# A decoder step on one core: the compressed-key branch, two sequences per weight block

## The chip, the cores and the metric

The kernel runs on one core of a Trainium2 chip. The metric is the device time of one execution in microseconds. The engines named below are PE (matrix products), PEld (its weight loads), DVE (vector), ACT (activations and copies), POOL (general purpose, here also the issuer of gathers and of some transfers) and SP (issuer of most transfers). Each engine executes its own instructions in program order and waits in place for whatever an instruction needs.

## The reference, cut to what matters

One inference step of a small trunk: a 512-token prompt and 8 decode sequences of 4 tokens go through a convolution module and a SwiGLU feed-forward layer (FFN), then through sparse attention and a second FFN. The part that the change rewrites is `compress` for the decode sequences. Each of the 8 sequences has 1024 cached rows in pages; every 32 rows are flattened with their 64 values (a vector of 2048), for keys (e=0) and values (e=1) and 4 heads, and pass a two-layer perceptron:

```python
def compress(kv_full, w_phi1, b_phi1, w_phi2, b_phi2, pe_cmp):
    blk = kv_full[:, :n * CMP_BLOCK].reshape(B, n, CMP_BLOCK, 2, KV_HEADS, HEAD_DIM)
    blk = blk + pe_cmp.transpose(1, 0, 2)[:, :, None, :]
    blk = blk.transpose(0, 1, 3, 4, 2, 5).reshape(B, n, 2, KV_HEADS, CMP_BLOCK * HEAD_DIM)
    hid = jax.nn.silu(jnp.einsum('bnegf,efh->bnegh', blk, w_phi1) + b_phi1[:, None, :])
    out = jnp.einsum('bnegh,ehd->bnegd', hid, w_phi2) + b_phi2[:, None, :]
```

Per sequence and e that is 32 blocks x 4 heads = 128 columns against a 2048 x 128 weight, so 16 weight blocks of 128 x 128, in fp32. The position term `pe_cmp` is the same for all columns; it is multiplied with the weights once and becomes part of the bias `bh`.

## The kernel before, in words

The program is written as one stream of calls per stage; a scheduler that ships with the language orders each engine's instructions by priority and by its own estimate of when inputs are ready. The stages that matter here, in order: the convolution (DVE chains of 31 taps, some channels on PE); its layer norm (`layer_norm_out`: the sum of the channels at L814 on PE, the centred rows `y` at L820 on DVE, their squares on ACT and the sums of these at L814 on PE, root, reciprocal, then `h_hi`/`h_lo` at L831/L832); the product with `w_pw2` (8 blocks of L183/L185 at 256 and 288 columns, called pw2 below); the norm before the FFN; and the first FFN with units j=0 to 7 (a gate and an up product, L183/L185 at 272 columns; the pair is joined at L915 on DVE, rounded at L921 on ACT, and the rest `a_lo` is made at L922 on POOL), then the product with the first part of `w_down` (called down below), which reads `a_hi` and `a_lo` of units 0 to 7 in turn, and so on. Slabs of `w_ada` (L451 load, L453 product) are strewn in between.

The compressed branch is a generator, `compress_steps`. All its steps are drawn in one go under a very low priority (`high_priority(-LATER)`) and behind the last tap of the convolution's DVE chains (`issue_after(self.last_step)`); MID is 24, the number of its steps, so all of it is drawn. By this the scheduler fills it into gaps of the stages above. Per sequence b and half hp: a gather on POOL (L1032, 1 MB into one of two `nat` tiles), two DVE transposes (L1045) into the `xt` tiles of keys and values; then per e a chain of 16 products (L1051: stationary weight block, 128 moving columns), for b=0 another 16 with one column for the bias (L1055), Silu on ACT (L1059), and a small second product (L1062 for keys, L1068 for values) with its bias on DVE (L1066, L1071); the values' rows go to DRAM from POOL (L1072). A PE call in fp32 shows as two instructions in the trace, so a chain is 32. The accumulators come from the two banks `t`.

Behind the branch, in the pool of SBUF that it gives back, the bias tables are made (`bias_tables`: L1092 and L1117 on PE, the transfers line_r, line_f and bs_d at L1099, L1096, L1121 on POOL), and then the selected and window keys are moved (`key_steps`: gather kr at L1032 on POOL into one of two tiles, v_d at L1301 on SP, transposes ktr at L1306 on DVE, kt_d at L1309 on SP; 24 steps of about 1 to 2 MB of traffic).

Of the kernel before, what the change touches and what calls it, by code (L numbers as in the profile page):

```python
# [7 lines left out]
F32 = mybir.dt.float32  # L8
F32R = mybir.dt.float32r
I32 = mybir.dt.int32  # L10
AF = mybir.ActivationFunctionType
# [14 lines left out]
G = 4  # L26
# [27 lines left out]
MID = 24  # L54
# [59 lines left out]
class Kernel:  # L114
# [883 lines left out]
    def compress_loads(self, pool):  # L998
# [21 lines left out]
        pe = pool.tile([P, P], F32, name="hk", bufs=2)[:, :HD]  # L1020
# [13 lines left out]
    def compress_steps(self, pool):  # L1034


        v, s, g, te = self.v, self.s, self.g, self.te
        self.compress_loads(pool)
        for b in range(NB):
            xts = [self.shift_pool.tile([P, 8, 8, 32], F32, name="xt", bufs=3) for _ in range(2)]  # L1040
            for hp in range(2):
                nat = pool.tile([P, 4, 512], F32, name="nat", bufs=2)
                self.load_rows(nat.rearrange("p t e -> p (t e)"), self.A["cache_kv_cmp"], hp, b)
                for e in range(2):
                    v.transpose(xts[e][:, hp * 4:hp * 4 + 4].rearrange("p s q n -> p s (q n)"), nat[:, :, e * 256:(e + 1) * 256])  # L1045
                yield
            for e in range(2):
                xv = xts[e].rearrange("p s (g h) n -> p h s g n", h=2)
                ph = self.bank()
                for c in range(16):  # L1050
                    te.matmul(ph[:, :P], self.w1[:, e, c // 2, c % 2], xv[:, c % 2, c // 2], start=c == 0, stop=c == 15)  # L1051
                if b == 0:
                    pb = self.bank()
                    for c in range(16):
                        te.matmul(pb[:, :1], self.w1[:, e, c // 2, c % 2], self.peT[:, c % 2, e * 8 + c // 2:e * 8 + c // 2 + 1],  # L1055
                                  start=c == 0, stop=c == 15)
                    v.tensor_scalar(self.bh[:, e:e + 1], pb[:, :1], self.b_phi1[:, e:e + 1], None, op0=ALU.add)
                hk = pool.tile([P, P], F32, name="hk", bufs=2)
                s.activation(hk, ph[:, :P], AF.Silu, bias=self.bh[:, e:e + 1])  # L1059
                po = self.bank()  # L1060
                if e == 0:
                    te.matmul(po[:, :P], self.w2k, hk, start=True, stop=True)  # L1062
                    pv = po[:, :P].rearrange("p (q g n) -> p q g n", q=2, g=2)
                    for g2 in range(2):
                        sl = slice(g2 * HD, (g2 + 1) * HD)
                        v.tensor_scalar(self.cks[sl, b], pv[sl, :, g2], self.b2k[sl], None, op0=ALU.add)  # L1066
                else:
                    te.matmul(po[:, :HD], hk, self.w2v, start=True, stop=True)  # L1068
                    cv = pool.tile([32, 256], F32, name="cv", bufs=1)
                    for gg in range(G):  # L1070
                        v.tensor_tensor(out=cv[:, gg * HD:(gg + 1) * HD], in0=po[gg * 32:(gg + 1) * 32, :HD], in1=self.b2v[:32], op=ALU.add)  # L1071
                    g.dma_start(self.vtail[b, 0:32], cv)  # L1072
            yield
        self.dump("cks", self.cks)
# [573 lines left out]
    def run(self):  # L1648
# [5 lines left out]
        with sbuf("const") as self.cp, sbuf("norm") as self.np, \  # L1654
# [17 lines left out]
            with sbuf("conv") as pool:  # L1672
# [18 lines left out]
                with tc.high_priority(-LATER):  # L1691
                    for _ in between:
                        pass
                    with tc.issue_after(self.last_step):
                        for _ in range(MID):
                            next(compress)
                    self.conv_states(pool)
# [120 lines left out]
```

## Time and profile before

| | us |
|---|---|
| median of 3 runs | 1673.56 (1667.45 to 1677.68) |
| the profiled execution's own time | 1666.48 |
| its span in the profile | 1664.7 |
| PE busy in that span | 1562.4 |
| DVE / ACT / POOL busy | 1109.1 / 696.1 / 230.5 |

Times inside the execution count from the start of the span. PE is busy for 94% of it, but the share differs by stage, and a busy PE may run at half its clock: the column PEclk is the granted clock as a share of 2.4 GHz, so a mean of 0.8 means that a part of the stretch ran at the lower level of 1.2 GHz. The chain of waits lists what ended last, step by step, with start and duration; "x32" there counts instructions, and the duration of a merged row over its count is the pace.

### The profile page before, as it was taken

To read this page: it belongs to the slowest core of one execution; us is meant where nothing else is said; L and a number is where in the kernel's file an instruction comes from. 1 tells how busy PE (TensorE), PEld (TensorE's weight loads), DVE (VectorE), ACT (ScalarE), POOL (GpSimd) and SP (SyncE) were. 2 spreads that over 40 slices of the span, in tenths; PEclk is the share of its full clock that TensorE was granted. 3 is DMA by queue.
4 is the path that set the end of the run, shared out by engine and by line. 5 is a ranking of instruction groups with operands and counts; after the bars stand their busy time and mean duration, and the time that the engine had idled before them with its cause. 6 is when DMAs were issued, how large, how long until landed. Compare 5 with 4: busy or idle time off the path is not lost.

```text
span 1664.7 us, 31621 instructions
## 1 busy us (share of the span) xinstructions
PE 1562.4 (94%) x12423; PEld 1372.3 (82%) x12423; DVE 1109.1 (67%) x2369; ACT 696.1 (42%) x1443; POOL 230.5 (14%) x270
## 2 busy tenths in 40 slices
PE   6989889999989978999999899999999999999997
PEld 3976468899979868999878677655699999999997
DVE  2899855464457877687656634867856864884865
ACT  5411145322132433155445322756746542652554
POOL 3254310111121112001120000000011110110010
PEclk8989888999999999999999999999999999999998
DMA  9729662653389999835689885847222472333231
GB/s 309 213 66 249 184 198 88 216 166 128 118 215 329 317 290 314 277 107 113 180 259 275 257 246 180 228 149 231 56 65 76 152 228 86 91 114 90 79 91 64
DMA packets 315568, 295.26 MB, mean 177 GB/s; under 512 B 16019, under 2 KB 275485, under 8 KB 311179
## 3 DMA queue, kind: packets, MB, share of 16 engines
q1 hardware_dynamic: 304507, 237.24, 48.3%
q0 software_dynamic: 10224, 55.47, 10.4%
q8 instruction: 98, 1.61, 0.4%
q10 hardware_dynamic: 688, 0.53, 0.1%
q14 instruction: 51, 0.42, 0.1%
HBM read 256.28 MB, written 45.48 MB: 181 GB/s over the span
## 4 chain that ended last, share of the span: by engine, by line
PE 65%; DMA 15%; DVE 12%; issue 4%; ACT 2%; SPq 1%; POOL 0%; ACTq 0%; DVEq 0%; POOLq 0%
PE g L185 16%; PE g L183 15%; PE g L247 10%; PE t L247 3%; DMA raw<-in_w_ada_dram 3%; PE t L155 3%; PE t L1051 3%; DMA raw<-in_w_gate_dram 2%; PE o L1532 2%; DVE wlo L196 2%; DVE y L770 2%; DMA raw<-in_w_down_dram 1%; PE a L453 1%; PE t L1381 1%; DVE wlo L170 1%
## 5 line engine op out<-in xcount | busy, mean ns | idle before, releaser
L169 ACT CAST whi<-raw 128x512 fp32r<-128x512 f32 x250 | 149.4, 605 | 394.1 <-PE g L185 287.1
L170 DVE TENSOR_TENSOR wlo<-raw,whi 128x512 fp32r<-128x512 f32 x250 | 174.9, 705 | 142.2 <-ACT whi L169 132.7
L183 PE MATMUL g<-h_hi,whi 128*128 128x256 f32 (+1 forms) x584 | 172.7, 297 | 12.8 <-DVE un L682 7.9
L185 PE MATMUL g<-h_lo,whi 128*128 128x288 f32 (+4 forms) x584 | 175.3, 300 | 0.6 <-DVE h_lo L577 0.6
L185 PE MATMUL g<-h_hi,whi 128*128 128x288 f32 (+4 forms) x584 | 174.9, 300 | 0.9 <-ACT h_hi L576 0.9
L185 PE MATMUL g<-h_hi,wlo 128*128 128x288 f32 (+4 forms) x584 | 174.5, 299 | 0.0
L183 PE MATMUL g<-h_lo,whi 128*128 128x256 f32 (+1 forms) x584 | 168.8, 289 | 0.4 <-DVE h_lo L562 0.4
L183 PE MATMUL g<-h_hi,wlo 128*128 128x256 f32 (+1 forms) x584 | 168.9, 289 | 0.0
L183 PEld LDWEIGHTS g<-h_hi,whi 128*128 128x128 f32 x584 | 113.1, 194 | 28.9 <-issue 17.0
L247 PE MATMUL g<-T,whi 128*128 128x272 f32 x656 | 126.9, 289 | 2.7 <-DVE ht L261 1.2
L195 ACT CAST whi<-s 128x512 fp32r<-128x512 f32 x128 | 79.4, 621 | 111.0 <-PE g L247 61.0
L183 PEld LDWEIGHTS g<-h_hi,wlo 128*128 128x128 f32 x584 | 113.0, 193 | 4.3 <-issue 4.2
L185 PEld LDWEIGHTS g<-h_hi,whi 128*128 128x128 f32 x584 | 113.1, 194 | 3.3 <-issue 2.1
L183 PEld LDWEIGHTS g<-h_lo,whi 128*128 128x128 f32 x584 | 113.1, 194 | 3.1 <-issue 2.4
L185 PEld LDWEIGHTS g<-h_lo,whi 128*128 128x128 f32 x584 | 112.4, 192 | 3.3 <-issue 2.3
L183 PE MATMUL g<-a_hi,whi 128*128 128x256 f32 (+1 forms) x372 | 107.1, 288 | 7.7 <-DVE x L641 3.1
L185 PEld LDWEIGHTS g<-h_hi,wlo 128*128 128x128 f32 x584 | 112.6, 193 | 1.2 <-issue 1.2
L185 PE MATMUL g<-a_hi,wlo 128*128 128x288 f32 (+1 forms) x372 | 110.5, 297 | 0.0
L185 PE MATMUL g<-a_hi,whi 128*128 128x288 f32 (+1 forms) x372 | 110.2, 297 | 0.0
L183 PE MATMUL g<-a_lo,whi 128*128 128x256 f32 (+1 forms) x372 | 105.2, 283 | 5.0 <-POOL a_lo L922 5.0
L185 PE MATMUL g<-a_lo,whi 128*128 128x288 f32 (+1 forms) x372 | 109.8, 296 | 0.0
L196 DVE TENSOR_TENSOR wlo<-s,whi 128x512 fp32r<-128x512 f32 x128 | 88.7, 697 | 26.4 <-ACT whi L195 22.3
(512 smaller groups left out, 4154.3 us busy)
## 6 DMA issues: line engine op xcount, KB each, us to landing
raw<-in_w_ada_dram SPq DMA_DIRECT2D x76, 512.0 KB
raw<-in_w_gate_dram SPq DMA_DIRECT2D x44, 512.0 KB
raw<-in_w_up_dram SPq DMA_DIRECT2D x44, 512.0 KB
raw<-in_w_down_dram SPq DMA_DIRECT2D x32, 512.0 KB
raw<-in_w_pw_dram SPq DMA_DIRECT2D x24, 512.0 KB
kt_d<-ktr SPq DMA_DIRECT2D x96, 128.0 KB
kt<-kt_d SPq DMA_DIRECT2D x24, 512.0 KB
xt<-in_w_ada_dram SPq DMA_DIRECT2D x20, 512.0 KB
```

Source lines behind the costliest of these rows:

```text
L155: self.te.transpose(out, in_, self.ident[:n, :n])
L169: self.s.copy(hi[:, :b - a], raw[:, a:b])
L170: self.v.tensor_tensor(out=lo[:, :b - a], in0=raw[:, a:b], in1=hi[:, :b - a].bitcast(F32), op=ALU.subtract)
L183: self.last_product = self.te.matmul(pg[:, 0, :split], a, b[:, i, :split], start=st, stop=sp).ins
L185: self.te.matmul(pg[:, 1, :tokens - split], a, b[:, i, split:tokens], start=st, stop=sp)
L195: self.s.copy(hi, src)
L196: self.v.tensor_tensor(out=lo, in0=src, in1=hi.bitcast(F32), op=ALU.subtract)
L247: self.te.matmul(out, a[:, i], b(i), start=first and i == 0 and j == 0, stop=i == 3 and j == 2, skip_group_check=not first)
L453: self.te.matmul(pa[32 * j:32 * j + 32, :256], self.cT[:, k, :], w[:, j * 256:(j + 1) * 256], start=k == 0, stop=k == KT - 1)
L770: self.last_step = v.scalar_tensor_tensor(out=ps, in0=x, scalar=w, in1=ps, op0=ALU.mult, op1=ALU.add).ins
L1051: te.matmul(ph[:, :P], self.w1[:, e, c // 2, c % 2], xv[:, c % 2, c // 2], start=c == 0, stop=c == 15)
L1532: te.matmul(po[rp * HD:(rp + 1) * HD, :256], self.vn[:, br, t, gg * HD:(gg + 1) * HD], pT[:, rp * 256:(rp + 1) * 256], start=br == 0 and t ...
```

## The change

Two sequences go through the branch together. Both gathers of a half are issued, the two sequences' transposes write one `xt` tile per half and e, and each weight block meets 256 columns in one call: 128 calls of 256 columns (L1065) take the place of 256 calls of 128. Two accumulators are held through both halves. Silu and the keys' second product take 256 columns at a time; the values' second product stays at 64 columns, twice. The bias is made first, by 32 calls with `peT` as the stationary side (one column) and the weights as 128 moving columns (L1042), a copy of the row on ACT and two transposes on PE. The tile `hk` has one buffer of twice the size in the place of two. MID goes away: the generator is still drawn whole at the same place, under the same priority. Line numbers behind the constants fall by one, those behind the branch rise by 12.

The diff:

```diff
--- before.py
+++ after.py
@@ -51,7 +51,6 @@
 STATE = 2
 LAST = KT - 1
 ORDER = (0, 1, 2, 3, 4, 5, 6, 7)
-MID = 24
 PE_CONV = (3, 4, 5, 6, 7)
 
 BUCKET_START = [16, 21, 27, 35, 46, 59, 77, 99, 128, 166, 216, 280, 363, 470, 609, 790]
@@ -1017,7 +1016,7 @@
         self.b2v = cp.tile([P, HD], F32, name="b2v")
         self.sy.dma_start(self.b2v, A["b_phi2"][1].rearrange("(o d) -> o d", o=1).broadcast_to([P, HD]))
         self.bh = cp.tile([P, 2], F32, name="bh")
-        pe = pool.tile([P, P], F32, name="hk", bufs=2)[:, :HD]
+        pe = pool.tile([P, 2, P], F32, name="hk", bufs=1)[:, 0, :HD]
         self.v.memset(pe, 0.0)
         src = A["pe_cmp"].rearrange("e (a s) d -> a e s d", a=4)
         for a in range(4):
@@ -1036,40 +1035,53 @@
 
         v, s, g, te = self.v, self.s, self.g, self.te
         self.compress_loads(pool)
-        for b in range(NB):
-            xts = [self.shift_pool.tile([P, 8, 8, 32], F32, name="xt", bufs=3) for _ in range(2)]
+
+        pb = self.bank()
+        for e in range(2):
+            for c in range(16):
+                te.matmul(pb[:1, e * P:(e + 1) * P], self.peT[:, c % 2, e * 8 + c // 2:e * 8 + c // 2 + 1], self.w1[:, e, c // 2, c % 2],
+                          start=c == 0, stop=c == 15)
+        row = pool.tile([P, 2, P], F32, name="hk", bufs=1)[:1]
+        s.copy(row, pb[:1, :2 * P].rearrange("p (e n) -> p e n", e=2))
+        pb = self.bank()
+        for e in range(2):
+            self.transpose(pb[:, e:e + 1], row[:, e])
+        v.tensor_tensor(out=self.bh, in0=pb[:, :2], in1=self.b_phi1, op=ALU.add)
+        yield
+
+        for b in range(0, NB, 2):
+            phs = [self.bank() for _ in range(2)]
             for hp in range(2):
-                nat = pool.tile([P, 4, 512], F32, name="nat", bufs=2)
-                self.load_rows(nat.rearrange("p t e -> p (t e)"), self.A["cache_kv_cmp"], hp, b)
+                nats = [pool.tile([P, 4, 512], F32, name="nat", bufs=2) for _ in range(2)]
+                for i in range(2):
+                    self.load_rows(nats[i].rearrange("p t e -> p (t e)"), self.A["cache_kv_cmp"], hp, b + i)
                 for e in range(2):
-                    v.transpose(xts[e][:, hp * 4:hp * 4 + 4].rearrange("p s q n -> p s (q n)"), nat[:, :, e * 256:(e + 1) * 256])
+                    xt = self.shift_pool.tile([P, 2, 4, 8, 32], F32, name="xt", bufs=3)
+                    for i in range(2):
+                        v.transpose(xt[:, i].rearrange("p s q n -> p s (q n)"), nats[i][:, :, e * 256:(e + 1) * 256])
+                    xv = xt.rearrange("p i s (g h) n -> p s h i g n", h=2)
+                    for c in range(8):
+                        k = 4 * hp + c // 2
+                        te.matmul(phs[e][:, :2 * P], self.w1[:, e, k, c % 2], xv[:, c // 2, c % 2], start=hp == 0 and c == 0, stop=hp == 1 and c == 7)
                 yield
             for e in range(2):
-                xv = xts[e].rearrange("p s (g h) n -> p h s g n", h=2)
-                ph = self.bank()
-                for c in range(16):
-                    te.matmul(ph[:, :P], self.w1[:, e, c // 2, c % 2], xv[:, c % 2, c // 2], start=c == 0, stop=c == 15)
-                if b == 0:
-                    pb = self.bank()
-                    for c in range(16):
-                        te.matmul(pb[:, :1], self.w1[:, e, c // 2, c % 2], self.peT[:, c % 2, e * 8 + c // 2:e * 8 + c // 2 + 1],
-                                  start=c == 0, stop=c == 15)
-                    v.tensor_scalar(self.bh[:, e:e + 1], pb[:, :1], self.b_phi1[:, e:e + 1], None, op0=ALU.add)
-                hk = pool.tile([P, P], F32, name="hk", bufs=2)
-                s.activation(hk, ph[:, :P], AF.Silu, bias=self.bh[:, e:e + 1])
+                hk = pool.tile([P, 2, P], F32, name="hk", bufs=1)
+                s.activation(hk.rearrange("p i n -> p (i n)"), phs[e][:, :2 * P], AF.Silu, bias=self.bh[:, e:e + 1])
                 po = self.bank()
                 if e == 0:
-                    te.matmul(po[:, :P], self.w2k, hk, start=True, stop=True)
-                    pv = po[:, :P].rearrange("p (q g n) -> p q g n", q=2, g=2)
+                    te.matmul(po[:, :2 * P], self.w2k, hk.rearrange("p i n -> p (i n)"), start=True, stop=True)
+                    pv = po[:, :2 * P].rearrange("p (i q g n) -> p i q g n", i=2, q=2, g=2)
                     for g2 in range(2):
                         sl = slice(g2 * HD, (g2 + 1) * HD)
-                        v.tensor_scalar(self.cks[sl, b], pv[sl, :, g2], self.b2k[sl], None, op0=ALU.add)
+                        v.tensor_scalar(self.cks[sl, b:b + 2], pv[sl, :, :, g2], self.b2k[sl], None, op0=ALU.add)
                 else:
-                    te.matmul(po[:, :HD], hk, self.w2v, start=True, stop=True)
-                    cv = pool.tile([32, 256], F32, name="cv", bufs=1)
-                    for gg in range(G):
-                        v.tensor_tensor(out=cv[:, gg * HD:(gg + 1) * HD], in0=po[gg * 32:(gg + 1) * 32, :HD], in1=self.b2v[:32], op=ALU.add)
-                    g.dma_start(self.vtail[b, 0:32], cv)
+                    for i in range(2):
+                        te.matmul(po[:, i * HD:(i + 1) * HD], hk[:, i], self.w2v, start=True, stop=True)
+                    for i in range(2):
+                        cv = pool.tile([32, 256], F32, name="cv", bufs=1)
+                        for gg in range(G):
+                            v.tensor_tensor(out=cv[:, gg * HD:(gg + 1) * HD], in0=po[gg * 32:(gg + 1) * 32, i * HD:(i + 1) * HD], in1=self.b2v[:32], op=ALU.add)
+                        g.dma_start(self.vtail[b + i, 0:32], cv)
             yield
         self.dump("cks", self.cks)
 
@@ -1692,8 +1704,8 @@
                     for _ in between:
                         pass
                     with tc.issue_after(self.last_step):
-                        for _ in range(MID):
-                            next(compress)
+                        for _ in compress:
+                            pass
                     self.conv_states(pool)
                 self.layer_norm_out(pool, acc, ada1)
             self.dump("x1", self.x)
```

The scheduler sets all engines' order anew. Three places:

PE, from the end of the convolution to the first product of pw2 (`ada_sb`, `raw,cT`: slabs of w_ada; `acc`, `sq`: the layer norm's sums; `g<-h_hi`: pw2). Before:

```order
L814 MATMUL g<-sq,ones 128x272 x14
L453 MATMUL a<-raw,cT 32x256 x4
L1062 MATMUL t<-hk,w2k 128x128
L1051 MATMUL t<-xt,w_1958 128x128 x6
L814 MATMUL g<-sq,ones 128x272 x2
L1051 MATMUL t<-xt,w_1958 128x128 x10
L1055 MATMUL t<-peT,w_1958 128x1 x6
L453 MATMUL a<-raw,cT 32x256 x4
L1055 MATMUL t<-peT,w_1958 128x1 x10
L453 MATMUL a<-raw,cT 32x256 x4
L183 MATMUL g<-h_hi,whi 128x256
```

and now:

```order
L1042 MATMUL t<-w_1958,peT 1x128 x8
L813 MATMUL g<-sq,ones 128x272 x2
L452 MATMUL a<-raw,cT 32x256 x4
L1042 MATMUL t<-w_1958,peT 1x128
L813 MATMUL g<-sq,ones 128x272 x2
L1042 MATMUL t<-w_1958,peT 1x128 x4
L154 MATMUL t<-c_small,hk 128x1 x2
L1065 MATMUL t<-xt,w_1958 128x256 x9
L452 MATMUL a<-raw,cT 32x256 x4
L1065 MATMUL t<-xt,w_1958 128x256 x13
L182 MATMUL g<-h_hi,whi 128x256
L184 MATMUL g<-h_hi,whi 128x288
```

Behind the norm's last sum there now stand 22 calls of 256 columns ahead of pw2, where 10 of 128 and 16 bias calls stood; the bias calls stand between the sums of squares, and nothing of the branch stands ahead of the first sum. Over the whole program the 256-column calls stand 22 ahead of pw2, 18 within it, 24 between it and the FFN, and 64 in the FFN ahead of down; the 128-column calls stood 32, 11, 37 and 176.

POOL, around the hand-over from the branch to the keys in the first FFN (`a_lo` rows are units 6 and 7 before, and units 5, 6 and 7 now). Before:

```order
L922 TENSOR_TENSOR a_lo<-ht,a_hi 128x544
L1099 DMA line_r<-lsb 512x1x320 x2
L1096 DMA line_f<-lsb 16x512 x2
L1121 DMA bs_d<-bs 4x32x394 x2
L1032 DMA kr<-in_cache_kv_sel_dram,rows_78 128x2048 x2
L922 TENSOR_TENSOR a_lo<-ht,a_hi 128x544
L1032 DMA kr<-in_cache_kv_sel_dram,rows_78 128x2048 x6
```

and now:

```order
L1111 DMA line_r<-lsb 512x1x320 x2
L1108 DMA line_f<-lsb 16x512 x2
L921 TENSOR_TENSOR a_lo<-ht,a_hi 128x544
L1133 DMA bs_d<-bs 4x32x394 x2
L1031 DMA kr<-in_cache_kv_sel_dram,rows_78 128x2048 x2
L921 TENSOR_TENSOR a_lo<-ht,a_hi 128x544
L1031 DMA kr<-in_cache_kv_sel_dram,rows_78 128x2048
L921 TENSOR_TENSOR a_lo<-ht,a_hi 128x544
L1031 DMA kr<-in_cache_kv_sel_dram,rows_78 128x2048 x7
```

Two gathers stood ahead of the last `a_lo` (unit 7); now three stand ahead of it, and two ahead of that of unit 6. On PE the first product of the bias tables stands 195 products of L183/L185 ahead of down now, and 78 before.

DVE, at the same place (`ht<-ht,g` joins a unit: unit 7 before, units 6 and 7 now). Before:

```order
L915 TENSOR_TENSOR ht<-ht,g 128x544
L949 TENSOR_TENSOR sg<-h_hi,h_lo 128x544
L170 TENSOR_TENSOR wlo<-raw,whi 128x512
L272 TENSOR_TENSOR sg<-sg 128x272
L273 SCALAR_TENSOR_TENSOR sg<-sg 128x272
L278 TENSOR_TENSOR h_lo<-sg,h_hi 128x272
L274 SCALAR_TENSOR_TENSOR sg<-sg 128x272
L949 TENSOR_TENSOR sg<-h_hi,h_lo 128x544
L170 TENSOR_TENSOR wlo<-raw,whi 128x512
L1306 STREAM_TRANSPOSE ktr<-kr 128x4x4x32 x2
```

and now:

```order
L914 TENSOR_TENSOR ht<-ht,g 128x544
L169 TENSOR_TENSOR wlo<-raw,whi 128x512
L1318 STREAM_TRANSPOSE ktr<-kr 128x4x4x32 x2
L169 TENSOR_TENSOR wlo<-raw,whi 128x512
L1318 STREAM_TRANSPOSE ktr<-kr 128x4x4x32 x2
L169 TENSOR_TENSOR wlo<-raw,whi 128x512
L277 TENSOR_TENSOR h_lo<-sg,h_hi 128x272
L948 TENSOR_TENSOR sg<-h_hi,h_lo 128x544
L271 TENSOR_TENSOR sg<-sg 128x272
L272 SCALAR_TENSOR_TENSOR sg<-sg 128x272
L169 TENSOR_TENSOR wlo<-raw,whi 128x512
L277 TENSOR_TENSOR h_lo<-sg,h_hi 128x272
```

The first transposes of the keys stood behind the join of unit 7; now two pairs stand between those of units 6 and 7.

## Rows read from the trace of the kernel before

**Rows 1.** The page, part 1: busy time and share of the span by engine.

```profile
PE 1562.4 (94%) x12423; PEld 1372.3 (82%) x12423; DVE 1109.1 (67%) x2369; ACT 696.1 (42%) x1443; POOL 230.5 (14%) x270
```

**Rows 2.** Windows by stage: length, busy (instructions) by engine, PEclk, DMA share, GB/s.

```profile
215.50:254.70 39.20, 33.52 (x216) 26.97 (x216) 19.43 (x27) 17.14 (x25) 2.56 (x3) 0.81 0.60 199
254.70:312.40 57.70, 57.66 (x462) 55.31 (x463) 28.00 (x57) 21.02 (x34) 0.57 (x1) 0.95 0.37 116
312.40:330.90 18.50, 16.48 (x128) 14.74 (x128) 10.65 (x21) 9.35 (x16) 4.91 (x5) 0.82 0.92 285
330.90:480.50 149.60, 148.47 (x1219) 141.64 (x1217) 79.06 (x138) 40.23 (x74) 29.43 (x36) 1.00 0.49 141
480.50:491.30 10.80, 5.78 (x48) 5.54 (x44) 4.50 (x9) 2.23 (x4) 3.38 (x3) 0.88 0.99 238
491.30:695.00 203.70, 185.00 (x1427) 172.51 (x1428) 150.76 (x253) 69.01 (x133) 26.37 (x22) 0.96 0.99 316
```

**Rows 3.** The same windows for the chains alone (L1051): PE, PEld, PEclk, DMA.

```profile
215.50:254.70 39.20, 10.98 (x64) 10.44 (x64) 0.81 0.60 199
...
312.40:330.90 18.50, 11.00 (x74) 10.88 (x74) 0.82 0.92 285
330.90:480.50 149.60, 43.70 (x355) 41.41 (x353) 1.00 0.49 141
```

**Rows 4.** The chain of waits, paces: start, duration, engine, tile, line, instructions.

```profile
228.16 2.57 PE t L1055 x24
243.12 0.93 PE g L814 x4
...
405.63 3.57 PE t L1051 x32
...
426.36 3.63 PE t L1051 x32
```

**Rows 5.** The chain of waits from the first slab to pw2.

```profile
222.26 0.94 PE a L453 x8
...
226.03 0.57 PE a L453 x8
...
227.24 0.92 PE g L814 x4
...
244.07 0.72 ACT rstd L825
...
248.29 2.31 DVE xt L1045 x2
...
254.74 0.58 PE g L183
```

**Rows 6.** The chain of waits, norm before the FFN and bias tables.

```profile
320.17 5.87 PE t L1051 x32
...
467.29 1.02 PE t L1092 x8
```

**Rows 7.** Timeline of POOL at the keys: start, us, instruction, idle before.

```profile
470.31 1.04 POOL L1096 DMA_DIRECT2D line_f<-lsb  x2
...
487.57 1.05 POOL L1032 DMA_INDIRECT kr<-in_cache_kv_sel_dram,rows  x1 [10.32 <-DMA line_f<-lsb]
488.93 0.98 POOL L1032 DMA_INDIRECT kr<-in_cache_kv_sel_dram,rows  x1 [0.30 <-issue]
489.93 1.35 POOL L922 TENSOR_TENSOR a_lo<-ht,a_hi 128x544 fp32r<-128x544 f32 x1
509.10 1.33 POOL L1032 DMA_INDIRECT kr<-in_cache_kv_sel_dram,rows  x1 [17.82 <-DVE x L643]
```

**Rows 8.** Timeline of PE, the resumed product of down.

```profile
491.33 0.58 PE L183 MATMUL g<-a_lo,whi 128*128 128x256 f32 x1 [5.05 <-POOL a_lo L922]
```

**Rows 9.** Timeline of DVE, the first transposes of the keys.

```profile
495.79 2.02 DVE L1306 STREAM_TRANSPOSE ktr<-kr 128x512 f32<-128x512 f32 x2 [6.03 <-DMA kr<-in_cache_kv_sel_dram,rows]
```

## The prediction

> **What bounds the kernel now.** I read the page's first part, then windows by stage, then the chain of waits inside two of the stages, and last the timelines of POOL, PE and DVE where the keys begin. The first part says PE: 94% busy [rows 1]. So time falls only where PE works less, idles less, or runs longer at the upper of its two levels (1.2 and 2.4 GHz). The windows [rows 2] say where that is possible. In the FFN (330.9 to 480.5) nothing is lost: 148.5 of 149.6 us busy at clock 1.00. Before pw2 (215.5 to 254.7) PE idles 5.7 us and its clock is 0.81; pw2's stage runs at 0.95; the norm's gap (312.4 to 330.9) has 2.0 us idle at 0.82. From 491.3 to 695, DMA is 0.99 busy and PE loses 18.7 us idle and 4% of its clock, 8.1 us more: 26.8 us. The branch's chains lie in all stages up to 480.5: in instructions 64, 74 and 355 of those windows [rows 3], the rest in pw2's stage. Wherever PE is full, what the branch costs it is paid one for one.
>
> **The chains.** 32 instructions take 3.57 to 3.63 us at full clock, 0.1125 each [rows 4]; 256 calls are 512 instructions, 57.6 us. No row shows an fp32 call with 256 columns and a full weight block. Bounds: the one-column bias calls move nothing yet take 2.57/24 = 0.107 per instruction; the norm's sums move 272 fp32 columns at 0.93/4 = 0.2325 [rows 4]. If only the weight load counted, 128 calls would take 256 x 0.1125 = 28.8 us (a saving of 28.8; the FFN's products, rounded to fp32r and one instruction each, do come at 0.127 with 272 columns, worked out below); at the price of 272 columns 59.5 us (a loss of 1.9). I take 0.2325 x 256/272 = 0.219, nearest in columns and type: 0.436 us per call, 55.8 us, a saving of 1.8. Half the calls, nearly the same time.
>
> The Trainium skill speaks for the low bound: "TensorE: Matmul & The Clock Gate", section "Back-to-back issue gap", gives a warm matmul N/2.4 + 2.5 ns, an estimate of 109 ns for 256 columns, and its section "LDWEIGHTS (loading the stationary operand)" P/1.2, 107 ns for 128. By both, the chains would cost about 28 us. The trace does not agree for this type: 0.2325 us at 272 columns is twice that formula.
>
> **The bias.** Still 32 calls, 64 instructions, 0.107 each by the weight load: 7 us before and after. A sum of 128 columns would be at most 0.1125, 0.4 us more. The row's copy on ACT and two transposes of one column lie beside the sums; the single `hk` orders ACT behind PE's second layer, which other products cover. The second layer moves the same columns: zero. `cv` still has one buffer, so the second sequence's adds on DVE wait for the first's transfer, in the FFN, where PE is not waiting for DVE; without that cover some 2 us, four times.
>
> **Up to pw2.** The order puts 56 bias instructions among the norm's sums where 32 stood, and takes 14 of the branch's other products away: 24 x 0.107 - 14 x 0.1125 = +1.0 us. DVE also makes `peT` behind the centred rows; between nothing and 2.3 us by the transposes of [rows 5]. I take the last sum 2.7 us later, near the top, since DVE is in use there: 245.8 for 243.12 [rows 4]. Against this, the transposes that stood between the reciprocal and `ht` (2.31 us, [rows 5]) leave that path, so `h_hi` is ready 0.4 later, at about 255.1. PE is later than that: behind the sum it has 4 bias calls (0.9), the row's detour (0.7), 22 calls (9.6) and a slab (0.57 [rows 5]): 245.8 + 0.9 + 11.8 = 258.5. pw2 thus begins 3.8 us later than at 254.74 [rows 5], with the idle time ahead of it filled: 22 new calls equal 44 old, where 32 were done.
>
> **pw2 and the norm's gap.** In pw2 18 new calls replace 11: 7.9 - 2.5 = +5.4. Without idle time ahead, the clock should stay up: 57.7 us at 0.95 hold 2.9 us to win [rows 2]; I count all, nothing is the other end. Then 24 calls for 37: 10.5 - 8.3 = +2.1; the second layer +0.4. In the gap the chain shows 32 instructions at 5.87 us instead of 3.6 [rows 6], 2.3 lost, and 2.0 idle [rows 2]; with more of the branch's work at hand both go: -4.3, nothing the other end. FFN at 330.9 + 3.8 + 5.4 - 2.9 + 2.1 + 0.4 - 4.3 = 335.4.
>
> **FFN to down.** 149.6 - 176 x 0.225 + 64 x 0.436 = 137.9: down begins at about 473.3 for 480.5, 7.2 us earlier.
>
> **The keys.** This is the step that decides what remains. Down's products read `a_lo` of unit 7, and PE resumes with it at 491.33 after waiting 5.05 us for POOL [rows 8], about 5.4 us of work into down. POOL was late because its gather waited 10.3 us for line_f, and a second gather and the `a_lo` followed [rows 7]. On PE the bias tables began at 467.29, 13.2 us and 78 products of the FFN ahead of down [rows 2, 6]; by the order 195 products stand there now. Outside the chains the FFN's instructions take (149.6 - 355 x 0.1125)/(1219 - 355) = 0.127 us [rows 2, 3], so the tables begin 13.2 + 117 x 0.127 = 28.1 us before 473.3, at about 445. Their path to the first gather was 487.57 - 467.29 = 20.3 us [rows 6, 7]: first gather at 465.3, 22 us earlier. But now the third gather too stands ahead of unit 7's `a_lo`, and it needs a `kr` tile back: it came 509.10 - 487.57 = 21.5 us after the first [rows 7]. With its own 1.33 and the `a_lo`'s 1.35, PE resumes at 465.3 + 24.2 = 489.5, 1.8 us earlier than before; of the 7.2 us won, 5.4 become a longer wait, 11 us for 5. Bounds: landing (495.79 - 487.57 = 8.2) and transposes (2.0 [rows 9]) alone would free a tile after 10.2 us, and then PE would not wait at all (-12); two turns, 43 us, would make it resume at 511 (+20). DVE's key transposes between the joins wait for that landing too, some 3 us that lie inside the same stall. I take the measured 21.5.
>
> **The DMA-bound stage.** Before, the first gather led the resumption by 3.8 us, now by 24.2: 20.4 of 203.7 us of traffic moves under FFN and stall, 10% of the 26.8 us lost: -2.7. Nothing, and nearly all 26.8, are the ends.
>
> **Sum.** -1.8 - 2.7 = -4.5 against the profiled execution's 1666.48: 1662.0. That execution stands 7.1 us under the median of the runs; against the median the forecast is **1669 us**.
>
> **Rivals.**
> A, nothing is won: the stage after 491 takes the earlier start back because weights and keys share a full DMA. For it: 0.99 [rows 2]. Against: traffic that moved earlier is gone from the stage. About 1674. Chance 0.18.
> B, the saturated stage is relieved: if weights are late only for want of bandwidth, 20 us of traffic done before frees up to 20 us. For it: the idle 18.7 us all lie where DMA is at 0.99 [rows 2]. Against: the keys' pace is set by two `kr` tiles, so they will stretch beside the weights as before. -17 to -26: 1648 to 1657. Chance 0.17.
> C, the change does for PE what the halved calls suggest, weight loads being the cost: -28.8 and part of B, about 1640. The 272-column row speaks against it. Chance 0.05. It is the time that the formulas of the Trainium skill would give.
> D, slower: POOL's third gather stands ahead of the last `a_lo`. It needs `kr` back, whose transfer to DRAM stands on SP behind weights, whose buffers come free only as PE moves on; and PE waits for that `a_lo`. Break-even is a third gather some 26.7 us after the first (4.5 us lost at 0.87); at two turns (43 us) +21.5, less 13% of it given back by the stage: +14 in all, 1688; it passes 1% from about 46 us. For it: 17.8 us of POOL's wait before that gather already [rows 7]. Against: the FFN's DMA is at 0.49 [rows 2], so this turn should be no slower than the measured one. 1678 to 1695. Chance 0.10.
> The forecast has 0.50, within 1661 to 1677.
>
> **How the numbers follow.** A measurement of this kernel tells 1% (16.7 us) from no change, no less. Faster by that, below 1656.8: most of B and all of C, 0.20. Slower, above 1690.3: half of D and a tail, 0.07. The rest, 0.73, is no change. The range leaves out C, the edge of B, and the worse half of D: 1650 to 1682. All term bounds but the chain's low one (C) and the keys' high one (D) lie within it.
>
> **What would show it.** Right: 256-column calls at about 0.436 us; pw2's first product near 258.5, the FFN's near 335, down's near 473; the first gather near 465 and PE then waiting some 11 us for unit 7's `a_lo`, with the third gather just ahead of it; idle time of the next 200 us a little below 18.7. Wrong: calls near 0.22 (C); a stage behind the resumption with less than 8 us idle (B); a third gather more than 27 us behind the first (D); the FFN's start not much later, or down's not earlier, which would break the account of the terms ahead of the keys.

## The result, and the profile after

The changed kernel takes 1654.16 us (median of 9 runs) where the kernel before takes 1670.92 in the same comparison: ratio 0.9907, 95% interval 0.9878 to 0.9936. One of the 9 runs of the kernel before took 5624.93 us and is left out of the ratio. Two further series gave 0.9893 (0.9866 to 0.9920) and 0.9899 (0.9870 to 0.9929). The forecast was 1669 with a range of 1650 to 1682. The time is inside the range, but outside 1661 to 1677, which had half of the chance: the gain of about 16 us, or 1%, is more than three times the 4.5 us that the sum gave.

The page's first part, after, beside [rows 1]:

```profile
PE 1555.1 (94%) x12161; PEld 1354.2 (82%) x12161; DVE 1109.4 (67%) x2360; ACT 693.8 (42%) x1435; POOL 233.6 (14%) x270
```

PE is busy for 7.3 us less, and for the same share of the span. Stages of the profiled execution, as in [rows 2] (length, then busy time and instructions by engine, granted clock, DMA share, GB/s); the stretches are the norm's sums up to pw2, pw2 with the norm's gap, the FFN, the hand-over and the DMA-bound stage:

```profile
230.58:264.26 33.68, 30.57 (x183) 20.73 (x179) 17.99 (x22) 12.83 (x18) 2.05 (x2) 0.97 0.35 100
264.26:340.81 76.55, 76.39 (x578) 69.80 (x576) 46.49 (x85) 27.50 (x45) 9.19 (x11) 1.00 0.64 199
340.81:478.30 137.49, 136.41 (x985) 125.70 (x985) 62.88 (x110) 37.20 (x64) 27.68 (x34) 1.00 0.52 152
478.30:492.57 14.27, 7.73 (x49) 7.08 (x45) 12.51 (x19) 3.12 (x6) 2.62 (x2) 0.87 0.87 261
492.57:690.00 197.43, 182.49 (x1384) 170.50 (x1385) 149.90 (x255) 70.15 (x135) 25.56 (x21) 0.95 0.99 308
```

pw2, its gap and the FFN now run with little idle time (0.2 and 1.1 us) and at a granted clock of 1.00. The pace of the chains, from the chain of waits (the row that answers to [rows 4]):

```profile
413.85 12.09 PE t L1065 x56
```

12.09/56 = 0.216 us per instruction, 0.432 per call: 55.3 us for all 128, where 57.6 stood. Calls near 0.22 us, the sign of rival C, are not there, so C is out. The formula of the Trainium skill ("TensorE: Matmul & The Clock Gate", "Back-to-back issue gap") gives an estimate of 0.109 us for 256 columns, half of the 0.216 us per instruction; the row does not agree.

PE up to pw2, from its timeline (start, us, instruction, idle before and what ended it; the rows answer to [rows 5]):

```profile
229.57 1.08 PE L452 MATMUL a<-raw,cT 128*32 128x256 f32 x8 [6.36 <-DMA raw<-in_w_ada_dram]
230.58 2.18 PE L813 MATMUL g<-acc,ones 128*128 128x272 f32 x4
234.27 2.10 PE L813 MATMUL g<-sq,ones 128*128 128x272 f32 x8 [0.88 <-ACT sq L821]
238.15 1.91 PE L1042 MATMUL t<-w,peT 128*1 128x128 f32 x16 [1.78 <-DVE peT L1026]
251.27 1.19 PE L813 MATMUL g<-sq,ones 128*128 128x272 f32 x4
264.26 0.47 PE L182 MATMUL g<-h_hi,whi 128*128 128x256 f32 x1
```

From the first sum (230.58) to the last (251.27) it takes 20.7 us where it took 15.9: 56 bias instructions now stand between them, at 0.115 us each (the 16 from 238.15 on take 1.84 us), and PE waits 1.78 us for `peT`.

The hand-over, on POOL, DVE and PE (the rows that answer to [rows 7, 8, 9]):

```profile
470.28 1.06 POOL L1031 DMA_INDIRECT kr<-in_cache_kv_sel_dram,rows  x1 [12.49 <-DMA line_f<-lsb]
...
472.64 1.40 POOL L921 TENSOR_TENSOR a_lo<-ht,a_hi 128x544 fp32r<-128x544 f32 x1
489.86 0.96 POOL L1031 DMA_INDIRECT kr<-in_cache_kv_sel_dram,rows  x1 [15.82 <-DVE sg L270]
490.85 1.67 POOL L921 TENSOR_TENSOR a_lo<-ht,a_hi 128x544 fp32r<-128x544 f32 x1
```

```profile
479.67 1.98 DVE L1318 STREAM_TRANSPOSE ktr<-kr 128x512 f32<-128x512 f32 x2 [13.37 <-DMA kr<-in_cache_kv_sel_dram,rows]
481.51 0.67 DVE L169 TENSOR_TENSOR wlo<-raw,whi 128x512 fp32r<-128x512 f32 x1
482.10 2.02 DVE L1318 STREAM_TRANSPOSE ktr<-kr 128x512 f32<-128x512 f32 x2
...
489.38 0.71 DVE L914 TENSOR_TENSOR ht<-ht,g 128x544 f32<-128x544 f32 x1
```

```profile
482.23 0.58 PE L182 MATMUL g<-a_hi,wlo 128*128 128x256 f32 x1 [3.17 <-DVE wlo L169]
490.82 0.39 PE L182 MATMUL g<-a_hi,whi 128*128 128x256 f32 x1 [2.14 <-ACT a_hi L920]
492.57 0.58 PE L182 MATMUL g<-a_lo,whi 128*128 128x256 f32 x1 [1.23 <-POOL a_lo L921]
```

The third gather does stand just ahead of the last `a_lo`, as forecast. But DVE is the one that is late: it sits 13.4 us before the first transposes of the keys, until their gather lands, and the join of unit 7 (`ht`, L914) stands behind them and behind all that piled up, so that it runs at 489.38, and only then can ACT make `a_hi` and POOL `a_lo`. PE's own first wait, 3.17 us for `wlo`, is for a row of DVE behind the same transposes.

Since one execution differs from another by several us, I cut every profile at the same instructions of PE. Two profiles of the kernel before, three of the change (us; a row ends at the first product of its stage; "resumption" is the first product with unit 7's `a_lo`, "attention" the first product on `cks`, "prompt" the first product `o<-pTp,vn` of the prompt's attention, so that the decode attention is the stretch to the prompt):

| stretch | before | change | forecast of the difference | measured (means) |
|---|---|---|---|---|
| first to last sum | 15.9, 14.3 | 20.7, 20.7, 21.7 | +2.7 | +5.9 |
| to pw2 | 11.8, 11.8 | 13.0, 13.0, 13.0 | +1.1 | +1.2 |
| to the FFN | 76.2, 75.5 | 76.6, 76.8, 76.6 | +0.7 | +0.8 |
| to down | 149.6, 149.4 | 137.5, 137.5, 137.5 | -11.7 | -12.0 |
| to the resumption | 10.8, 10.7 | 14.3, 13.4, 13.5 | +5.4 | +3.0 |
| to the attention | 361.0, 365.1 | 359.0, 361.1, 352.8 | -2.7 | -5.4 |
| to the prompt | 200.8, 200.4 | 197.9, 194.3, 192.9 | 0 | -5.6 |
| to the end | 611.5, 609.2 | 609.9, 608.7, 609.2 | 0 | -1.1 |

The measured column sums to -13.2. Up to the resumption it is -1.1, and 12.1 us are gained behind it.

### The profile page after: what moved, and what is told of

It is laid out like the page before. It is cut to its first block, busy times and chain, and to the rows that moved or that the text cites. A ratio compares the mean times of both kernels' runs of the same rounds, so it can differ in the third digit from the quotient of the medians.

```text
span 1659.3 us, 31075 instructions
## 1 busy us (share of the span) xinstructions
PE 1555.1 (94%) x12161; PEld 1354.2 (82%) x12161; DVE 1109.4 (67%) x2360; ACT 693.8 (42%) x1435; POOL 233.6 (14%) x270
## 4 chain that ended last, share of the span: by engine, by line
PE 66%; DMA 14%; DVE 12%; issue 4%; ACT 2%; SPq 2%; POOL 0%; DVEq 0%; ACTq 0%; POOLq 0%
PE g L184 17%; PE g L182 16%; PE g L246 9%; PE t L1065 3%; PE t L246 3%; PE t L154 3%; DVE wlo L195 2%; PE o L1544 2%; DMA raw<-in_w_ada_dram 2%; DVE y L769 2%; PE a L452 2%; DVE wlo L169 1%; DMA raw<-in_w_down_dram 1%; DMA kt_d<-ktr 1%; PE t L1393 1%
## 5 line engine op out<-in xcount | busy, mean ns | idle before, releaser
L182 PE MATMUL g<-h_hi,whi 128*128 128x256 f32 (+1 forms) x584 | 172.1, 296 | 11.1 <-DVE un L681 8.1
L182 PEld LDWEIGHTS g<-h_hi,whi 128*128 128x128 f32 x584 | 112.7, 193 | 23.3 <-issue 13.4
L246 PEld LDWEIGHTS g<-T,whi 128*128 128x128 f32 x656 | 104.0, 190 | 8.6 <-ACT whi L194 5.2
```

What stands on the lines that cost most here:

```text
L182: self.last_product = self.te.matmul(pg[:, 0, :split], a, b[:, i, :split], start=st, stop=sp).ins
L246: self.te.matmul(out, a[:, i], b(i), start=first and i == 0 and j == 0, stop=i == 3 and j == 2, skip_group_check=not first)
```

## The experiments

The diffs show the lines that matter; `...` stands for others. Intervals behind a ratio are 95%, and every ratio is to the kernel before.

**Twice the same.** The kernel before against itself: 

> The kernel before, unchanged, to learn how far two executions of one program differ. All theories: ratio 1.000 within 0.003. Its second profile tells which of the differences between the two first profiles are chance: in the first 210 us, where both programs issue the same instructions in the same order, the changed kernel's profiled execution was 4.6 to 6.2 us behind, in transfers; if that is chance, two executions of this program differ there by several us too.

Ratio 0.9994 (0.9976 to 1.0012). Its profile was 6.2 us behind the first one at 180 us, as far as that of the change, where all three run the same instructions: the lag of the change there was chance.

The change again, twice: 

> The changed kernel, unchanged, for a second profile and more runs. Ratio 0.988 to 0.994. Theory H (the gain comes from the order at the hand-over: the branch is done earlier, tables and gathers start earlier, and the stage that is bound by DMA loses less): lag of PE against the kernel before, counted from 215 us, again about +4 to +6 at the FFN, -7 to -8 at the start of down, -2 to -4 at its resumption, -4 to -6 at 695 us. If the lead after 695 us (another 4 to 5 us in the first profiles) is systematic, it shows here again; if it is chance, it does not.

> The changed kernel again, beside the next three on the same chip, and for a third profile. Ratio 0.987 to 0.993; from 500 to 680 us and from 860 to 1010 us it gains several us each on the order of before, as in its first two profiles.

0.9893 and 0.9899. The lead behind 695 us is there in all three profiles (the table's last row but one): systematic.

**Structure or columns.**

```diff
-  te.matmul(phs[e][:, :2 * P], self.w1[:, e, k, c % 2], xv[:, c // 2, c % 2], ...)
+  for i in range(2):
+      te.matmul(phs[e][:, i * P:(i + 1) * P], self.w1[:, e, k, c % 2], xv[:, c // 2, c % 2, i], ...)
```

> As the changed kernel, but each 256-column call is two calls of 128 columns with the same weight block, into the halves of the accumulator. The scheduler then puts the last a_lo behind two gathers again and the tables 89 products ahead of down (78 before, 195 in the change), and 149 of the 128-column calls into the FFN (176 before, 64 of 256 in the change). Theory H: most of the gain goes, ratio 0.994 to 1.000. Theory C (the gain is that of the chains' own price, fewer weight loads): the chains cost 57.6 instead of 55.3 us, 2.3 us more than the change, ratio 0.992 to 0.993 by price alone.

0.9920 (0.9895 to 0.9946). Theory H's figure is missed. Theory C's is met, but C accounts only for the 2.3 us of the columns' price (1657.45 us against 1655.28, a difference within the noise). Without one 256-column call most of the gain remains, and its first gather leads the resumption by 3.8 us, as before: neither the columns nor the early keys carry most of it. What is left in common with the change is the order: its FFN took 141.9 us, the stretch to the prompt 194.1. From the resumption to the attention it took 364.9 us, as long as before.

**The bias alone**, put into the kernel before (a row of 128 columns first, the one-column calls gone):

```diff
+  te.matmul(pb[:1, e * P:(e + 1) * P], self.peT[...], self.w1[...], ...)   # 32, ahead of the branch
-  te.matmul(pb[:, :1], self.w1[...], self.peT[...], ...)                   # 32, in the branch
```

> The kernel before with one part of the change: the bias first, as a row of 128 columns, its copy and two transposes, ahead of the branch; the 128-column chains, xt tiles and gathers are as before. The order at the hand-over stays that of before (tables 77 products ahead of down, two gathers ahead of the last a_lo), and so does the order on DVE in the attention. Theory H (order at the hand-over) and theory K (below): nothing, ratio 0.998 to 1.002. If the gain lay in the bias: 0.990 to 0.994.

0.9989 (0.9962 to 1.0015): nothing, as forecast.

**Tables and keys late.**

```diff
+  for _ in range(13):
+      yield
   with sbuf("bias") as pool2:
-      self.bias_tables(pool2)
-      yield
+      with tc.issue_after(self.last_pool):
+          self.bias_tables(pool2)
...
-          yield
+          if n > 13:
+              yield
```

> As the changed kernel with its 256-column calls, but bias tables and keys are drawn behind unit 6 of the FFN: the tables stand 72 products ahead of down on PE (78 before, 195 in the change), the last a_lo behind two gathers. The chains are untouched. Theory H: gathers start some 15 to 20 us later than in the change, near 485 us, and the gain falls to 3 to 8 us, ratio 0.995 to 0.998. Theory C or any theory in which the place of the keys does not matter: ratio 0.990 to 0.992 as the change.

0.9980 (0.9957 to 1.0003), the figure of theory H, but not for its reason: the slabs of `w_ada`, drawn in the same loop, crowded ahead of unit 7, PE waited 3.9 us for them and 2.9 for weights, its granted clock was 0.84 in the last 32 us ahead of down, and the FFN took 147.3 us, 9.8 more than in the change. At the hand-over the last `a_lo` stands behind two gathers and their wait for line_f, as before:

```profile
505.36 0.58 PE L182 MATMUL g<-a_lo,whi 128*128 128x256 f32 x1 [5.71 <-POOL a_lo L921]
```

From the resumption to the attention it took 355.9 us, no more than the change. The run says nothing against late keys.

**The order in the attention.**

```diff
+  if k == 0 and st == 0:
+      self.first_max = red.ins
...
+  with self.tc.issue_after(self.first_max):
       v.tensor_tensor(out=fm[...], in0=pk[:, 0:2, :C0], ...)
```

> The changed kernel, but in the decode attention the first ht of keys and values must stand behind the reduction that waits for bs on DVE, as it does in the kernel before; in the change it stands one row ahead of it. Theory K: in the profiles PE waits 6.7 and 8.2 us there before and 7.1 and 4.8 after, and the lead grows by 3 to 4 us between 860 and 1000 us; with the old order these come back, ratio 0.991 to 0.993 where the change has 0.989 to 0.991. Rival: the lead there has another cause (transfers that come earlier), ratio as the change.

0.9922 (0.9893 to 0.9951): theory K's figure, but the interval overlaps the change's and cannot tell the two apart. The stretch to the prompt can: it took 194.2 us, as short as the change's. Theory K falls: that one row of DVE is not the cause.

**The last `a_lo` ahead of the third gather on POOL**, DVE's transposes left where they were (third and later steps of the keys drawn behind unit 7):

```diff
-  next((keys, ada)[n % 2], None)
+  if n % 2 == 0 and 4 <= n < 14:
+      held += 1
+  else:
+      next((keys, ada)[n % 2], None)
+  if n == 14:
+      for _ in range(held):
+          next(keys, None)
```

> The changed kernel, but the third and later steps of the keys are drawn behind unit 7 of the FFN: on POOL both last a_lo stand ahead of the third gather. The tables stay early (185 products ahead of down). In the attention DVE has the old order again (the reduction that waits for bs ahead of the first ht), which by theory K costs 3 to 4 us. Theory H: PE's idle time at the hand-over (6.5 us in the change) falls to 0 to 2 us, 4 to 6 us earlier at 500 us, of which the DMA-bound stage takes back about 13%; with K's loss about the change's time, ratio 0.988 to 0.992. Rival (the DMA-bound stage takes all back): equal at 695 us, ratio 0.991 to 0.994.

0.9900 (0.9871 to 0.9928). POOL, DVE and PE in its profile:

```profile
490.97 1.68 POOL L921 TENSOR_TENSOR a_lo<-ht,a_hi 128x544 fp32r<-128x544 f32 x1 [13.19 <-ACT a_hi L920]
```

```profile
481.98 2.01 DVE L1318 STREAM_TRANSPOSE ktr<-kr 128x512 f32<-128x512 f32 x2 [5.80 <-DMA kr<-in_cache_kv_sel_dram,rows]
...
485.54 2.00 DVE L1318 STREAM_TRANSPOSE ktr<-kr 128x512 f32<-128x512 f32 x2
...
489.51 0.71 DVE L914 TENSOR_TENSOR ht<-ht,g 128x544 f32<-128x544 f32 x1
```

```profile
492.70 0.58 PE L182 MATMUL g<-a_lo,whi 128*128 128x256 f32 x1 [0.93 <-POOL a_lo L921]
```

POOL was free for 13.2 us and waited for `a_hi`; the join on DVE, behind the two pairs of transposes, ran at 489.51, and PE resumed at 492.70, 12.6 us behind the start of down (change: 13.4 to 14.3). The gather on POOL was not the bound.

**Half of the calls left out** (`for c in range(0, 8, 2)`; the kernel then sums over half of the weight blocks only):

> The changed kernel without every second 256-column call: 64 of 128 are left out (half of the sum over the weight blocks). At the price read from the second profile, 0.216 us per instruction, that is 27.6 us of PE. Where PE is the bound from 240 to 480 us, it is paid one for one up to the hand-over: down begins 20 to 28 us earlier. If the keys' transfers then set the pace (their gathers can start earlier only as the tables do), part is given back: total ratio 0.972 to 0.980. Theory that chains fill idle time of PE: under 10 us, ratio 0.984 or more.

0.9913 (0.9881 to 0.9946): 27.6 us of PE's work less, and no time gained against the change; 0.972 to 0.980 is missed. In its profile 6.2 us of them are left at the resumption (255.7 us from the first sum for 261.9). PE there:

```profile
471.92 0.57 PE L182 MATMUL g<-h_hi,whi 128*128 128x272 f32 x1 [9.29 <-DVE ht L914]
487.87 0.39 PE L182 MATMUL g<-a_hi,whi 128*128 128x256 f32 x1 [1.59 <-ACT a_hi L920]
489.65 0.38 PE L182 MATMUL g<-a_lo,whi 128*128 128x256 f32 x1 [1.26 <-POOL a_lo L921]
```

Two joins now wait behind the keys on DVE, and 9.3 us of what PE saves are spent in the first wait. Another 9 us were spent before: pw2 to the FFN took 85.7 us for 76.6.

**The keys held until the last `a_lo`**, tables early:

```diff
-  next((keys, ada)[n % 2], None)
+  if n % 2 or n > 14:
+      next((keys, ada)[n % 2], None)
+  elif n == 14:
+      with tc.issue_after(self.last_pool):
+          for _ in range(8):
+              next(keys, None)
```

> The changed kernel, but the gathers and transposes of the keys are held until the last a_lo of unit 7 has been issued on POOL; the bias tables stay early. Nothing of the keys stands ahead of a join or an a_lo any more. Theory H2 (the hand-over of the change costs about 6.5 us of waiting, for key transposes on DVE and a gather on POOL, while the early keys gain little): the wait falls under 2 us, PE is 4 to 6 us earlier at 500 us and the run 3 to 6 us faster than the change, ratio 0.985 to 0.988. Rival (early keys pay for the wait, as the first form of theory H said): the keys start some 8 to 12 us later, the DMA-bound stage gains less, and the time is that of the change or 2 to 4 us above it.

1645.44 us, 0.9849 (0.9822 to 0.9877): faster than both kernels, 9.4 us under the change in the same comparison (1654.86). DVE, POOL and PE:

```profile
482.45 0.71 DVE L914 TENSOR_TENSOR ht<-ht,g 128x544 f32<-128x544 f32 x1
```

```profile
483.93 1.67 POOL L921 TENSOR_TENSOR a_lo<-ht,a_hi 128x544 fp32r<-128x544 f32 x1 [15.62 <-ACT a_hi L920]
485.75 1.08 POOL L1031 DMA_INDIRECT kr<-in_cache_kv_sel_dram,rows  x1 [0.16 <-issue]
```

```profile
485.65 0.39 PE L182 MATMUL g<-a_lo,whi 128*128 128x256 f32 x1 [1.11 <-POOL a_lo L921]
```

From down to the resumption it took 6.9 us instead of 13.7: PE idles 1.1 us there, and its granted clock is 1.00 for 0.87 in the change's first profile. That is 6.8 of the 9.4 us. Counted from down, the first gather comes 14 to 15 us later than in the change, level with the resumption, and still the way to the attention is 356.1 us (change: 352.8 to 361.1). Early keys gain nothing that these profiles show, and their wait on DVE is a loss.

Held keys, and half of the calls left out:

> As the run before this one, without every second 256-column call (64 of 128 left out, half of the sum over the weight blocks), 27.6 us of PE. With the same calls left out and keys early the time was that of the change. If that was the hand-over's waiting (9.3 us for a join of DVE behind key transposes), more of the 27.6 us now shows: 10 to 18 us faster than the change. If PE idles in the FFN for other reasons or the DMA-bound stage takes it back, it stays within 4 us of the change.

1632.45 us, 0.9776 (0.9749 to 0.9803), 13 us under the run before and 22.4 under the change, more than the 10 to 18 expected. 48 of the 64 missing calls were in the FFN (16 stand there for 64), which is 48 x 0.432 = 20.7 us; the FFN took 117.4 us for 135.9, 18.5 less, and PE no longer waits at the hand-over. Ahead of the FFN the calls cost little: without half of them pw2 to the FFN took 85.2 us for 76.6, since PE then waits (3.3 us for `h_hi`, 2.3 for `h_lo`, 2.0 for `hk`).

Held keys in the kernel before:

> The kernel before with the keys drawn behind unit 7: the last a_lo stands ahead of all gathers, chains and bias as before. It removes the wait of 5.05 us at the start of down; the gathers start no earlier than before. Theory H2: 2 to 5 us faster than before, ratio 0.997 to 0.999; if the place of the keys is what the change gained by, nothing, ratio 0.999 to 1.002.

0.9924 (0.9900 to 0.9948), more than forecast. From down to the attention it took 367.0 us for 371.8 and 375.8. So the wait of [rows 8] could have been saved without the change. From down to the resumption the profile takes 5.6 us for 10.8 and 10.7; the profiled execution took 1668.18 us, 8 us above the median of its runs, so it does not show where the rest of the gain lies. On top of held keys the change still gives 0.9849/0.9924 = 0.9924.

## Why the prediction was right, and where it was wrong

The time is right as a range, not as a sum. At the resumption the change is 1.1 us ahead, where the forecast had 1.8; errors of +3.2 us between the sums and -2.4 at the hand-over cancel, which is luck. Behind the resumption it gains 12.1 us for 2.7: the terms there were mis-sized, and the experiments do not show what makes most of that gain. They show what it is not, and that the hand-over costs 7 us that need not be paid.

- **Chains.** Right: 0.432 us per call for 0.436, 2.3 us saved for 1.8. (Twice the 0.219 of the prediction is 0.438, which makes the saving 1.6.)
- **Bias.** Right in size: 0.115 per instruction for 0.107, a little over the bound of 0.1125, and alone it moves nothing. The reason given does not hold for the new calls: their weight load of one column takes 84 ns where that of 128 took 192, and the pace is still that of 128 moving columns. The loads before and after (minimum, median and maximum in ns):

```profile
L1055 PEld LDWEIGHTS t<-peT,w x64: 186/192/335, 227.8 to 250.4; 128*128 128x128 f32 x64
```

```profile
L1042 PEld LDWEIGHTS t<-w,peT x64: 79/84/84, 238.1 to 253.0; 128*1 128x1 f32 x64
```

- **Up to pw2.** The step was right in direction and mis-sized: +5.9 us for +2.7 between the sums. "Between nothing and 2.3" for `peT` left out that PE waits for it (1.8) and that the bias and slabs stand between single sums. pw2, the FFN and down began at 264.3, 340.8 and 478.3 for 258.5, 335 and 473; some 3 us of that lie ahead of the first sum.
- **pw2, gap, FFN.** Right within 0.3 us for the FFN, and for pw2 and the gap together. Apart these two miss: pw2 took 61.3 us for 57.7 (57.1 in the second profile before), some 4.0 more where 2.5 was forecast, and the gap 15.2 for 18.4, 3.2 less for 1.8. With work at hand the idle time and the half clock of [rows 2] do go: both run at 1.00, with 0.2 us idle.
- **Keys.** The places were right to within a few us once chance ahead of 215 us is allowed for: tables 29.7 us ahead of down (28.1), first gather 21.7 behind them (20.3), third 19.6 behind the first (21.5), resumption 14.3 us behind down's start (16.2). PE waited 6.5 us (3.17, 2.14 and 1.23) where 11 was forecast. The cause was wrong. "The third gather too stands ahead of unit 7's `a_lo`" is so, but moving it changed nothing; the sentence "some 3 us that lie inside the same stall" named the true one, the transposes on DVE, as the minor. Holding the keys off both engines gave 9.4 us.
- **The DMA-bound stage.** -5.4 for -2.7, counted to the attention. The sign of the forecast is there: in the 200 us behind the resumption PE idles 14.9, 17.0 and 12.4 us where it idled 18.7 and 21.0. The mechanism is not borne out: "20.4 of 203.7 us of traffic moves under FFN and stall" is not needed, since three runs with 256-column calls whose first gather leads the resumption by 4.1 us at most (held keys, held keys with half of the calls, late tables) took 353.9 to 356.1 us. It is not excluded either: the split calls, with a lead of 3.8 us, took 364.9, and the change's own profiles differ by 8 us in this stretch. What the profiles show is that PE's wait for split weights (`wlo`) falls, from 9.9 and 15.8 us before to 5.4, 5.8 and 2.9, while that for `sg` rises from 0.7 to between 1.7 and 5.8. PE's waits for `wlo` in 500 to 700 us (total, times, longest), in the second profile before:

```profile
PE g L247 <- DVE wlo L196: 10.1, 4, 5.7
PE t L247 <- DVE wlo L196: 5.7, 3, 5.3
```

and in the first after:

```profile
PE t L246 <- DVE wlo L195: 2.9, 1, 2.9
PE g L246 <- DVE wlo L195: 2.5, 3, 2.1
```

The longest of before, in its chain of waits:

```profile
622.27 6.81 DMA kt_d<-ktr
629.10 0.69 DVE wlo L196
```

A transfer of the keys to DRAM ends, and then DVE makes the weights' low half: again work of the keys ahead of PE's on DVE. Which difference in the order spares the change this wait was not tried apart.

- **The attention.** Nothing stood in the sum for the stretch to the prompt, and that was wrong by 5.6 us: the order changes that far behind the edit. Four profiles with the order of before (the kernel twice, the bias alone, the held keys) take 200.1 to 202.2 us for this stretch, all ten profiles with two sequences per block 192.9 to 198.3. PE's waits there, before:

```profile
PE g L155 <- DVE ht L1208: 6.7, 1, 6.7
PE b L1445 <- DMA vs<-in_cache_kv_win_dram: 2.3, 1, 2.3
```

and after:

```profile
PE b L1457 <- DVE os_lo L1475: 7.1, 1, 7.1
PE b L1457 <- DMA vs<-in_cache_kv_win_dram: 1.3, 2, 0.9
```

The long wait has another name but the same source. DVE waits in place for the transfer of `bs`, and the rows that PE needs (`ht`, `os_lo`) stand behind it; before and after:

```profile
920.29 0.19 DVE L1342 CUSTOM_DVE_ANT_0 pc<-t,bs 128x32 f32<-128x32 f32 x1 [8.58 <-DMA bs<-bs_d]
```

```profile
921.75 0.19 DVE L1354 CUSTOM_DVE_ANT_0 pc<-t,bs 128x32 f32<-128x32 f32 x1 [7.35 <-DMA bs<-bs_d]
```

All 14 profiles have this wait: 8.6 to 10.5 us on DVE and 6.7 to 8.7 on PE in the four, 4.2 to 8.0 and 4.0 to 7.2 in the ten. What follows it takes 128.8 to 132.2 us in the four and 124.4 to 128.4 in the ten. So part of the 5.6 us is a shorter wait for `bs`, and the larger part comes behind it; which row of the order makes either stays open, since the one that was tried did not.

- **Rivals.** The time is that of B (1648 to 1657), but B's sign, less than 8 us idle, is missing, and its mechanism, traffic done early, is the one not borne out. A, nothing won, falls with the measured ratio. D's place (POOL) was not the bound. "Wherever PE is full, what the branch costs it is paid one for one" holds in the FFN, and only where the hand-over does not take it back.

The profiles account for 13 of the 16 us; the rest is within what single executions differ by.

## What to carry to other kernels

When work is moved earlier, look on every in-order engine for what now stands ahead of the critical instruction and waits for a transfer: here it was a transposition on DVE, not the next gather on POOL, and holding a few steps back gave more than half as much again as the change. Calls with twice the columns do not halve the time of an fp32 chain whose time already goes by its columns (here 0.1125 us per instruction at 128, 0.216 at 256, 0.2325 at 272). A new schedule moves stages that the edit does not touch; cut the profiles at the same instructions to see which.

## What the runs showed of the hardware

DVE waits in place: with a transposition at its head that waits 13.4 us for a gather, the join of unit 7 ran 11.1 us after down's start (489.38 - 478.30); with the keys held it ran 3.7 us after it (482.45 - 478.78). The Trainium skill ("PSUM — Partial Sum Buffer", "Engine vs sequencer instructions") says that "ScalarE/VectorE/GpSimdE queues are strict FIFO"; the trace agrees for DVE. A weight load of one column took 84 ns against 192 for 128, with no gain in pace, 0.115 us for 0.107.
